# The last eight odd U chunks computed ahead, sixteen early gathers, and the gathered block closed at chunk 121

## The chip, the cores and the metric

The kernel runs on one core of a Trainium2 chip. The core has a matrix engine (TensorE, PE in the profile, PEld its weight loads), a vector engine (DVE), a scalar engine (ACT), GpSimd (POOL), and SP, which mostly issues DMA transfers. Each engine works through its own queue in order; semaphores make one wait for another. The metric is the time of one execution in microseconds (us) on the device.

## The reference, cut to what matters

One decoder block for 512 tokens of width 1024: attention and gated linear attention beside each other, then an expert layer, each behind a norm. The change touches the expert layer alone. For each token and each of 8 heads the 16 best of 16384 experts are picked (`expert`, `gates`), and

```
def block(args):
    xb, eb, gb = args                      # 128 tokens, 128 experts each
    ub = jnp.take(u, eb, axis=0)
    hid = jax.nn.gelu(jnp.einsum('tkd,td->tk', ub, xb)) * gb
    vb = jnp.take(v, eb, axis=0)
    return jnp.einsum('tk,tkd->td', hid, vb)
```

Behind it the result is scaled by a gate, added to the residual, normed and written out.

## The kernel before

The 512 tokens are four blocks of 128. Three of them (0, 1, 2) are computed **densely**: every expert for every token, with the gates as a matrix that is mostly zero. The fourth (`GB`, block 3) is computed by **gathers**: for each of its 128 places (16 experts of 8 heads) one indirect DMA fetches a row of `u` per token (gu) and one a row of `v` (gv).

The dense part goes through 128 chunks of 128 experts. For a chunk c there is

- a **U chunk** (`u_part`): ACT rounds the chunk of u to its high part (`uc..h`), DVE subtracts to get the low part (`uc..l`, called lo, L65), PE makes 24 matmuls of 128x368 into `ph` (L69 to L71; the last 16 of the 384 tokens take another way), ACT takes the gelu (L705) into `ge`.
- a **V chunk** (`v_part`, `v_matmuls`): ACT and DVE split v in the same way (`vc..h`, `vc..l`), DVE multiplies the gelu by the gates (L1169), ACT and DVE split the product into `Ah` (L1173) and `Al` (L1174), and PE adds 18 matmuls of 128x512 into the six accumulators `acc`.

The gelu of an odd chunk stays in SBUF (a ring of six) until its V chunk; that of an even chunk is written to DRAM (`gsp`) and read back for its V chunk (`gel`, two even chunks in one load).

Three stages follow each other after the front part (attention, mixers, query heads, to 403 us). In the **gate stage** (403 to about 714 us) PE builds the gate matrix from one-hot matrices (`pg`, L918) for the blocks one after the other, 8 places (q) to a block, and writes it to DRAM (`Gd`, read back as `gr`, eight chunks to a block of 1.5 MB). DVE is busy there with the one-hots. The 64 even U chunks (`AHEAD`) are woven in, by a running sum of the costs of DVE and PE. The first 8 gathers of u are done there too: each is issued at one place of the third block and its dot (`gather_u`, L1003) follows at the next. In the **V stage** (to 1503 us) each pair of V chunks has one odd U chunk, 8 chunks ahead (`LEAD`), until these are used up at chunk 119; the remaining gathers are spread evenly over chunks 0 to 123 (`gather_to`). The sum over gv is kept on DVE (`gacc`, L1016). After every eighth gu ACT takes the gelu of `hid` (L1006) and DVE multiplies it by the gates (hg, L1007). The last four V chunks (`LAST`) are done block by block, so that a block's accumulators are ready one after the other, and in the **tail** `finish` scales, adds, norms and writes each block (L1192 to L1203), the gathered block first.

The order of each engine's instructions is made ahead of time by a scheduler that simulates the program; DVE and POOL keep the written order in the gate stage, POOL also after it.

Of the kernel before, what the change touches and what calls it, by code (L numbers as in the profile page):

```python
# [46 lines left out]
def peer_block_kernel(ctx: ExitStack, tc: tile.TileContext, a: dict, out: bass.AP):  # L47
# [951 lines left out]
    def gather_u(s):  # L999
# [4 lines left out]
        if s % 8 == 7:  # L1004
            sl = slice(s - 7, s + 1)
            last_gelu["hg"] = nc.scalar.activation(hg[:, sl], hid[:, sl], AF.Gelu)  # L1006
            nc.vector.tensor_tensor(hg[:, sl], hg[:, sl], gg_g[:, sl], OP.mult)  # L1007
# [141 lines left out]
    def v_part(c):  # L1149
        if c % 2 == 0:  # L1150

            v_part.raw = dn.tile([P, 2, D], F32, tag="vraw", bufs=2, name=f"v{c}") if c else raw([P, 2, D], "v0")
            nc.sync.dma_start(v_part.raw, vPc[c:c + 2].rearrange("c i d -> i c d"))
        if c == 0:
            gates_of(0)
# [2 lines left out]
        if c % CG == 2 and c + CG < P:
# [2 lines left out]
        if c % 2 == 0:
            if c % 4 == 0:
                v_part.ge = dnA.tile([P, 2, TU], F32, tag="gel", bufs=2, name=f"gel{c}")
                nc.sync.dma_start(v_part.ge, gsp[c // 2:c // 2 + 2].rearrange("c p t -> p c t"))
            ge = v_part.ge[:, c // 2 % 2].rearrange("p (g t) -> p g t", g=NGU)
# [130 lines left out]
```

## Time and profile before

| | us |
|---|---|
| median of 3 runs | 1525.87 (1524.41 to 1526.83) |
| profiled execution | 1523.26 |
| its span | 1521.5 |
| front part and query heads | 0 to 403 |
| gate stage | 403 to 714 |
| V stage | 714 to 1503 |
| tail | 1503 to 1521.5 |

A time is that of the whole execution; the span runs from the first to the last instruction that the profiler recorded. In the profile an engine's busy share is over the whole span. A row of the timeline gives the start in us, the duration, engine, line, operation, tiles with their shapes, and in brackets how long the engine had been idle before and what ended it. A row of DMA issues gives the size and the median time from issue to landing.

### The profile page before, as it was taken

Reading aid. Unit: us, or ns where it says so; the run is one execution under the profiler, and the core shown is the slowest. Engines: PE = TensorE matmul, PEld = TensorE weight load, DVE = VectorE, ACT = ScalarE, POOL = GpSimd, SP = SyncE. Lnnn points to the kernel's source line nnn. Section 1 sums busy time; section 2 is a strip of 40 time slices with the busy share of each in tenths; the row PEclk is TensorE's granted clock in tenths of the full one; section 3 lists DMA queues with packets and bytes.
Section 4 is the critical chain, followed back from the end, with each engine's and each line's share of the span. In section 5 each row is a group of like instructions: output and inputs, shape, how many; then the busy total and the mean of one; then the engine's idle time right before and its main releaser. Section 6 shows DMA issues by size and latency. Waiting matters only on the chain.

```text
span 1521.5 us, 24401 instructions
## 1 busy us (share of the span) xinstructions
PE 1460.3 (96%) x9387; PEld 1301.7 (86%) x9387; DVE 1251.6 (82%) x2389; ACT 677.7 (45%) x1072; POOL 482.2 (32%) x344
## 2 busy tenths in 40 slices
PE   4999989899999999999999999999999999999995
PEld 3787877888999999999888888888888888888884
DVE  7578657689999999996778878787878878788998
ACT  5545486533344665765333333333333333333332
POOL 1000000145505220222334434453535434454461
PEclk9999999999999999999999999999999999999997
DMA  9253535462446997899999989989999898998894
GB/s 349 99 208 115 175 106 191 152 215 92 140 171 207 305 314 229 257 295 330 411 408 335 334 317 345 357 322 333 343 349 344 326 339 344 357 335 291 312 356 157
DMA packets 158004, 417.04 MB, mean 274 GB/s; under 512 B 11312, under 2 KB 78144, under 8 KB 145472
## 3 DMA queue, kind: packets, MB, share of 16 engines
q1 hardware_dynamic: 107296, 258.18, 47.5%
q0 software_dynamic: 39312, 144.20, 25.9%
q10 hardware_dynamic: 11280, 13.11, 2.5%
q8 instruction: 73, 1.20, 0.3%
q14 instruction: 43, 0.35, 0.1%
HBM read 374.01 MB, written 41.42 MB: 273 GB/s over the span
## 4 chain that ended last, share of the span: by engine, by line
PE 89%; DVE 4%; ACT 3%; DMA 2%; issue 2%; SPq 0%; DVEq 0%; POOL 0%; ACTq 0%; POOLq 0%
PE ph L71 11%; PE ph L69 11%; PE acc L70 11%; PE acc L69 11%; PE ph L70 11%; PE acc L71 11%; PE pg L918 4%; PE pq L69 2%; PE pq L71 2%; PE pq L70 2%; PE pj L71 1%; PE pj L69 1%; PE pj L70 1%; DMA gu<-in_u_dram,ix_u 1%; PE pn L69 1%
## 5 line engine op out<-in xcount | busy, mean ns | idle before, releaser
L993 POOL DMA_INDIRECT gu<-in_u_dram,ix_u x128 | 191.4, 1495 | 314.4 <-DVE gacc L1016 128.8
L1011 POOL DMA_INDIRECT gv<-in_vP_dram,ix_v x128 | 176.8, 1381 | 216.2 <-DVE gu L1003 163.9
L1173 ACT ACTIVATE Ah<-gr 128x384 fp32r<-128x384 f32 x128 | 67.1, 525 | 308.6 <-PE acc L70 305.0
L1016 DVE SCALAR_TENSOR_TENSOR gacc<-gv,hg,gacc 128x1024 f32<-128x1024 f32 x127 | 162.8, 1282 | 0.2
L1003 DVE SCALAR_TENSOR_TENSOR gu<-gu,h2n 128x1024 f32<-128x1024 f32 x128 | 156.0, 1220 | 0.7 <-DMA gu<-in_u_dram,ix_u 0.7
L705 ACT ACTIVATE ge<-ph 128x368 f32<-128x368 f32 x128 | 59.9, 468 | 152.8 <-PE ph L71 152.7
L1174 DVE TENSOR_TENSOR Al<-gr,Ah 128x384 fp32r<-128x384 f32 x128 | 71.0, 556 | 66.4 <-ACT Ah L1173 66.2
L920 ACT ACTIVATE gs<-pg 128x512 f32<-128x512 f32 x96 | 94.1, 1114 | 3.8 <-PE pg L918 2.8
L1066 POOL IOTA iot<- 128x256 bf16 x1 | 1.5, 1540 | 282.2 <-DVE h2Tl L680 282.2
L911 DVE TENSOR_TENSOR o<-o,gp 128x3072 bf16<-128x3072 bf16 x48 | 84.0, 1755 | 0.4 <-PE pg L918 0.4
L959 POOL DMA_INDIRECT spr<-in_u_dram,spix x16 | 40.6, 2535 | 105.6 <-DVE spr L964 61.3
L918 PE MATMUL pg<-o,o 128*128 128x128 bf16 x1152 | 72.7, 218 | 0.5 <-ACT gs L920 0.5
L918 PEld LDWEIGHTS <-o 128*128 128x128 bf16 x1152 | 66.2, 97 | 6.0 <-issue 0.7
L895 DVE TENSOR_TENSOR o<-iot,t 128x2048 bf16<-128x2048 bf16 x48 | 58.4, 1223 | 2.4 <-PE pg L918 2.4
L1169 DVE TENSOR_TENSOR gr<-ge,gr 128x368 f32<-128x368 f32 x64 | 34.5, 540 | 23.3 <-ACT ge L705 23.3
L217 DVE SCALAR_TENSOR_TENSOR macc<-wa,scs,macc 128x1024 f32<-128x1024 f32 x28 | 38.8, 1385 | 5.1 <-DMA wa<-in_w_ada_dram 4.8
L1169 DVE TENSOR_TENSOR gr<-gel,gr 128x368 f32<-128x368 f32 x64 | 31.9, 535 | 2.9 <-DMA gr<-Gd 2.9
L70 PE MATMUL pq<-h2Tl,wq_0h 128*128 128x512 f32 (+1 forms) x80 | 27.9, 349 | 1.2 <-DVE h2Tl L680 1.2
L69 PE MATMUL pq<-h2Th,wq_0h 128*128 128x512 f32 (+1 forms) x80 | 28.0, 352 | 1.0 <-ACT qha L758 1.0
L71 PE MATMUL pq<-h2Th,wq_1l 128*128 128x512 f32 (+1 forms) x80 | 28.1, 352 | 0.0
L70 PE MATMUL pq<-h2Tl,wq_1h 128*128 128x512 f32 (+1 forms) x80 | 28.1, 352 | 0.0
L69 PE MATMUL pq<-h2Th,wq_1h 128*128 128x512 f32 (+1 forms) x80 | 28.0, 350 | 0.0
(2608 smaller groups left out, 5028.3 us busy)
## 6 DMA issues: line engine op xcount, KB each, us to landing
u<-in_uT_dram SPq DMA_DIRECT2D x64, 1024.0 KB, 8.3
v<-in_vP_dram SPq DMA_DIRECT2D x64, 1024.0 KB, 7.5
Gd<-gs SPq DMA_DIRECT2D x23, 1024.0 KB, 8.1
gr<-Gd SPq DMA_DIRECT2D x15, 1536.0 KB, 11.0
wa<-in_w_ada_dram SPq DMA_DIRECT2D x20, 1024.0 KB, 6.3
gsp<-ge ACTq DMA_DIRECT2D x64, 184.0 KB, 4.6
gel<-gsp SPq DMA_DIRECT2D x32, 368.0 KB, 4.8
wi<-in_w_in_dram SPq DMA_DIRECT2D x9, 1024.0 KB, 6.2
```

The costliest lines, as they stand in the source:

```text
L69: nc.tensor.matmul(acc, lh, rh, start=start, stop=False)
L70: nc.tensor.matmul(acc, lh, rl, start=False, stop=False)
L71: return nc.tensor.matmul(acc, ll, rh, start=False, stop=stop)
L911: nc.vector.tensor_tensor(o2, o12[:, :, 1, None].to_broadcast([P, H, 3, P, 2]), gp3[:, g0:g0 + H, :, None].to_broadcast([P, H, 3, P, 2]), ...
L918: nc.tensor.matmul(pt[:, i, :], o12[:, g, 0, :, r], o2[:, g, m, :, r], start=(m == 0), stop=(m == 2))
L920: nc.scalar.activation(gs[:, :, t0 + 4 * f:t0 + 4 * f + 4].rearrange("p b a -> p a b"), pt, AF.Copy)
L993: nc.gpsimd.indirect_dma_start(out=ur, out_offset=None, in_=a["u"], in_offset=bass.IndirectOffsetOnAxis(ap=ix_u[:, s:s + 1], axis=0))
L1003: nc.vector.scalar_tensor_tensor(ur, ur, 1.0, h2n, op0=OP.mult, op1=OP.mult, accum_out=hid[:, s:s + 1])
L1011: nc.gpsimd.indirect_dma_start(out=vr, out_offset=None, in_=a["vP"], in_offset=bass.IndirectOffsetOnAxis(ap=ix_v[:, s:s + 1], axis=0))
L1016: nc.vector.scalar_tensor_tensor(gacc, vr, hg[:, s:s + 1], gacc, op0=OP.mult, op1=OP.add)
L1173: nc.scalar.activation(grp(Ah), A, AF.Copy)
L1174: nc.vector.tensor_tensor(grp(Al), A, grp(Ah), OP.subtract)
```

## The change

- Eight odd U chunks, 113, 115 to 127 (`ODD_AHEAD`, m = 28 to 31), join those computed ahead in the gate stage: 72 in place of 64. Their gelus are spilled to `gsp`, which is laid out anew, and read back as `gel1`.
- 16 gathers of u are done in the gate stage in place of 8. They are issued in pairs, at the last place of the second block and the first seven of the third; the two dots of a pair come one place later. The product hg of the first 16 is no longer made right behind ACT's gelu but at the next pair (`weigh`).
- The other gathers are spread over chunks 0 to 119 (`LAST_G`) in place of 0 to 123, by a cost of 4.0 for a V chunk of a pair with a U chunk and 2.3 for one of a pair without. The sum gv no longer starts ten places behind gu.
- The gathered block is closed (`finish(GB, ...)`), and ACT's table for the last norms loaded, at chunk 121, not behind the loop.
- The load of V chunk 0 and the first load of `gel` go to GpSimd's DMA queue, behind the first block of gates; they were on SP's.
- The load of the second block of gates is issued at chunk 4, no longer at chunk 2.

```diff
-AHEAD = tuple(range(0, P, 2))
+ODD_AHEAD = tuple(range(28, 32))
+AHEAD = tuple(c for m in range(P // 4) for c in (4 * m, 4 * m + 2) + ((4 * m + 1, 4 * m + 3) if m in ODD_AHEAD else ()))
...
-        if c % 2 == 0:
-            nc.scalar.dma_start(gsp[c // 2], gef)
+        if c in AHEAD:
+            nc.scalar.dma_start(gsp[c // 4, c % 2, c // 2 % 2], gef)
...
-    EARLY = 8
+    EARLY = 16
...
             last_gelu["hg"] = nc.scalar.activation(hg[:, sl], hid[:, sl], AF.Gelu)
+            waiting.append(sl)
+            if s >= EARLY:
+                weigh()
+
+    waiting = []
+
+    def weigh():
+        while waiting:
+            sl = waiting.pop()
             nc.vector.tensor_tensor(hg[:, sl], hg[:, sl], gg_g[:, sl], OP.mult)
...
-    VLAG = 10
-    gathers = [(s * 0.88 / NS, gather_u, s) for s in range(NS)]
-    gathers += [((s + VLAG) / (NS + VLAG), gather_v, s) for s in range(NS)]
+    gathers = [(-1, gather_u, s) for s in range(EARLY)]
+    gathers += [((s - EARLY) * 0.88 / (NS - EARLY), gather_u, s) for s in range(EARLY, NS)]
+    gathers += [((s + 0.5) / NS, gather_v, s) for s in range(NS)]
...
-    third_block = {0: [ahead(0, 1)]}
-    for q in range(1, EARLY):
-        third_block[q] = [dots_of(q - 1, 1), ahead(q, 1)]
-    third_block[EARLY - 1] += [dots_of(EARLY - 1, 1)]
+    third_block = {}
+    places = [(second_block, q) for q in range(7, 8)] + [(third_block, q) for q in range(P // TG)]
+    for i, (block, q) in enumerate(places):
+        pieces = block.setdefault(q, [])
+        if i:
+            pieces.append(dots_of(2 * i - 2, 2))
+        if i < EARLY // 2:
+            pieces.append(ahead(2 * i, 2))
...
+            if c == 0:
+                gates_of(0)
             v_part.raw = dn.tile([P, 2, D], F32, tag="vraw", bufs=2, name=f"v{c}") if c else raw([P, 2, D], "v0")
-            nc.sync.dma_start(v_part.raw, vPc[c:c + 2].rearrange("c i d -> i c d"))
-        if c == 0:
-            gates_of(0)
+            (nc.sync if c else nc.gpsimd).dma_start(v_part.raw, vPc[c:c + 2].rearrange("c i d -> i c d"))
...
-        if c % CG == 2 and c + CG < P:
+        if c % CG == (2 if c > CG else 4) and c + CG < P:
...
-                v_part.ge = dnA.tile([P, 2, TU], F32, tag="gel", bufs=2, name=f"gel{c}")
-                nc.sync.dma_start(v_part.ge, gsp[c // 2:c // 2 + 2].rearrange("c p t -> p c t"))
+                v_part.ge[c % 2] = dn.tile([P, 2, TU], F32, tag=f"gel{c % 2}", bufs=2 - c % 2, name=f"gel{c}")
+                (nc.sync if c else nc.gpsimd).dma_start(v_part.ge[c % 2], gsp[c // 4, c % 2].rearrange("c p t -> p c t"))
...
-    LEAD = 8
+    LEAD, LAST_G = 8, 120
+    share = [4.0 if c + 1 + LEAD < P and c + 1 + LEAD not in AHEAD else 2.3 for c in range(0, P, 2)]
+    cost = [share[c // 2] for c in range(LAST_G)]
...
-        if c % 2 == 0 and c + 1 + LEAD < P:
+        if c % 2 == 0 and c + 1 + LEAD < P and c + 1 + LEAD not in AHEAD:
             u_part(c + 1 + LEAD)
...
-        gather_to(len(gathers) * (c + 1) // (P - LAST))
+        weigh()
+        gather_to(EARLY + int((len(gathers) - EARLY) * sum(cost[:c + 1]) / sum(cost) + 1e-6))
+        if c == LAST_G + 1:
+            with tc.issue_after(last_gelu["u"].ins), tc.issue_after(last_gelu["hg"].ins):
+                nc.scalar.preload_act_table_set("natural_log_exp_and_others")
+            finish(GB, [gacc[:, 0:512], gacc[:, 512:1024]])
...
-    with tc.issue_after(last_gelu["u"].ins), tc.issue_after(last_gelu["hg"].ins):
-        nc.scalar.preload_act_table_set("natural_log_exp_and_others")
-    finish(GB, [gacc[:, 0:512], gacc[:, 512:1024]])
```

The order in which the engines take their work moves at three places.

ACT at the transition from the gate stage to the V stage, before (`ge9` is the gelu of the last U chunk ahead of the V stage, a name's last number only tells tiles apart):

```order
L705 ACTIVATE ge9_8344<-ph9_8319 128x368
L64 ACTIVATE vc0h_8350<-v0_8346 128x1024
L1173 ACTIVATE Ah0_8357<-gr0_8348 128x384
L64 ACTIVATE vc1h_8379<-v0_8346 128x1024
L1173 ACTIVATE Ah1_8384<-gr0_8348 128x384
```

and with the change:

```order
L706 ACTIVATE ge9_8633<-ph9_8608 128x368
L65 ACTIVATE vc0h_8639<-v0_8637 128x1024
L65 ACTIVATE vc1h_8675<-v0_8637 128x1024
L65 ACTIVATE uc11h_8708<-u9_8602 128x1024
L65 ACTIVATE vc2h_8741<-v2_8739 128x1024
L1189 ACTIVATE Ah0_8646<-gr0_8635 128x384
L1189 ACTIVATE Ah1_8680<-gr0_8635 128x384
```

Ah0, which PE's first V matmul reads, has three more operations ahead of it; PE has two matmuls of U chunk 11 between U chunk 9 and that first V matmul.

DVE in the chunks without U, from the lo of chunk 115 to that of chunk 116, with the change (L1185 is the product with the gates, L1190 Al, L1026 gacc, L1004 a dot):

```order
L66 TENSOR_TENSOR vc115l_14323<-v114_14288,vc115h_14322 128x1024
L1190 TENSOR_TENSOR Al117_14397<-gr14_14012,Ah117_14396 128x384
L1185 TENSOR_TENSOR gr15_14290<-gel120_14492,gr15_14290 128x23x16 x2
L1185 TENSOR_TENSOR gr15_14290<-gel124_14634,gr15_14290 128x23x16 x2
L1185 TENSOR_TENSOR gr15_14290<-gel121_14521,gr15_14290 128x23x16 x2
L1004 SCALAR_TENSOR_TENSOR gu124_13910,hid_2439<-gu124_13910,h2n_2430 128x1024
L1190 TENSOR_TENSOR Al118_14429<-gr14_14012,Ah118_14428 128x384
L1026 SCALAR_TENSOR_TENSOR gacc_8473<-gv109_13940,hg_2440,gacc_8473 128x1024
L1004 SCALAR_TENSOR_TENSOR gu125_13943,hid_2439<-gu125_13943,h2n_2430 128x1024
L1026 SCALAR_TENSOR_TENSOR gacc_8473<-gv110_13977,hg_2440,gacc_8473 128x1024
L1190 TENSOR_TENSOR Al119_14459<-gr14_14012,Ah119_14458 128x384
L1004 SCALAR_TENSOR_TENSOR gu126_14007,hid_2439<-gu126_14007,h2n_2430 128x1024
```

Twelve rows (fifteen operations) stand here between two lo subtractions; the products of chunks 120, 121, 122, 123, 124 and 126 are made in one go, four chunks or more ahead of their use.

ACT in the tail, before (rf1y and rf2y are the roots of blocks 1 and 2, L81 and L82 a logarithm and an exponential, y1 the rows of block 1):

```order
L81 ACTIVATE rf1y_14741<-rf1m_14740 128x1
L82 ACTIVATE rf1y_14741<-rf1y_14741 128x1
L81 ACTIVATE rf2y_14791<-rf2m_14790 128x1
L82 ACTIVATE rf2y_14791<-rf2y_14791 128x1
L1200 ACTIVATE y1_14730<-y1_14730,rf1y_14741 128x512 x2
```

and with the change:

```order
L82 ACTIVATE rf1y_14757<-rf1m_14756 128x1
L83 ACTIVATE rf1y_14757<-rf1y_14757 128x1
L82 ACTIVATE rf2y_14807<-rf2m_14806 128x1
L1218 ACTIVATE y1_14746<-y1_14746,rf1y_14757 128x512 x2
L83 ACTIVATE rf2y_14807<-rf2y_14807 128x1
```

The scaling of y1 now stands ahead of the last step of block 2's root.

More of the change, by code (lines that the diff above doesn't have):

```diff
@@ L687, in second_norm @@
                 nc.scalar.activation(h2n[:, half * 512:(half + 1) * 512], pb, AF.Copy)
-    gsp = dr.tile([len(AHEAD), P, TU], F32, name="gsp")
+    gsp = dr.tile([P // 4, 2, 2, P, TU], F32, name="gsp")
     ges, last_gelu = {}, {}
@@ L1105, in peer_block_kernel @@
                     6: [gate_parts(SB)], 7: [gate_rest(SB)]}
-    third_block = {0: [ahead(0, 1)]}
-    for q in range(1, EARLY):
-        third_block[q] = [dots_of(q - 1, 1), ahead(q, 1)]
-    third_block[EARLY - 1] += [dots_of(EARLY - 1, 1)]
+    third_block = {}
[6 more added lines that the diff above has]
+            pieces.append(ahead(2 * i, 2))
+    assert EARLY == 2 * len(places) - 2
     work = chain(route_heads(), *head, woven(0, rows, first_block), woven(1, rows, second_block),
@@ L1112, in peer_block_kernel @@
     NL_U = len(AHEAD) - LAST_U
-    DVE_ALL = 11 + 4 * 7.6 + 3 + 1.15 * TS + 2.82 * 2 * NGRP + 9 + 1.14 * (NL_U - WQ_U)
+    DVE_ALL = 11 + 4 * 7.6 + 3 + 1.15 * TS + 2.82 * 2 * NGRP + 1.15 * EARLY + 1.14 * (NL_U - WQ_U)
     PE_ALL = 1.4 * 2 * NGRP + 3 + UCOST * (NL_U - WQ_U)
@@ L1150, in v_part @@
         if c % 2 == 0:
+            if c == 0:
+                gates_of(0)
             v_part.raw = dn.tile([P, 2, D], F32, tag="vraw", bufs=2, name=f"v{c}") if c else raw([P, 2, D], "v0")
[L1153 to L1155 removed]
+            (nc.sync if c else nc.gpsimd).dma_start(v_part.raw, vPc[c:c + 2].rearrange("c i d -> i c d"))
         if c % CG == 0:
             v_part.g = gates_of.next
[L1158 removed]
+        if c % CG == (2 if c > CG else 4) and c + CG < P:
             gates_of(c // CG + 1)
         vh, vl = hilo(v_part.raw[:, c % 2], [P, D], f"vc{c}", nc.vector)
[L1161 to L1165 removed]
+        if c in AHEAD:
+            if c % 4 < 2:
+                v_part.ge[c % 2] = dn.tile([P, 2, TU], F32, tag=f"gel{c % 2}", bufs=2 - c % 2, name=f"gel{c}")
+                (nc.sync if c else nc.gpsimd).dma_start(v_part.ge[c % 2], gsp[c // 4, c % 2].rearrange("c p t -> p c t"))
+            ge = v_part.ge[c % 2][:, c // 2 % 2].rearrange("p (g t) -> p g t", g=NGU)
         else:
@@ L1175, in v_part @@
         return c, Ah, Al, vh, vl
+    v_part.ge = {}
     def v_matmuls(parts, blocks=range(len(DENSE)), qs=(0, 1)):
@@ L1214, in peer_block_kernel @@
         v_matmuls([parts])
-        gather_to(len(gathers) * (c + 1) // (P - LAST))
+        weigh()
+        gather_to(EARLY + int((len(gathers) - EARLY) * sum(cost[:c + 1]) / sum(cost) + 1e-6))
[3 more added lines that the diff above has]
+            finish(GB, [gacc[:, 0:512], gacc[:, 512:1024]])
         if c == 16:
```

## The prediction

> **What bounds the kernel now.** I read the page first, for the engine that fills the span; then the chain of waits; then the windows, one per stage, since the shares are means over stages with different limits; then the waits of TensorE (PE).
>
> ```profile
> span 1521.5 us, 24401 instructions
> PE 1460.3 (96%) x9387; PEld 1301.7 (86%) x9387; DVE 1251.6 (82%) x2389; ACT 677.7 (45%) x1072; POOL 482.2 (32%) x344
> PE 89%; DVE 4%; ACT 3%; DMA 2%; issue 2%; SPq 0%; DVEq 0%; POOL 0%; ACTq 0%; POOLq 0%
> ...
> 403.00:714.30 311.30, 309.48 (x2601) 303.28 (x2600) 289.35 (x446) 181.23 (x234) 73.18 (x40) 1.00 0.79 255
> 714.30:734.40 20.10, 20.10 (x122) 19.89 (x120) 7.48 (x12) 4.28 (x7) 8.47 (x9) 1.00 1.01 413
> 734.40:736.40 2.00, 0.10 (x1) 0.00 (x0) 0.96 (x2) 1.87 (x4) 0.00 (x0) 1.00 1.02 406
> 736.40:740.90 4.50, 4.49 (x13) 3.54 (x14) 4.50 (x7) 4.04 (x6) 1.68 (x1) 0.62 1.03 418
> 742.40:1438.00 695.60, 695.60 (x3412) 612.16 (x3412) 570.19 (x748) 251.66 (x355) 305.93 (x217) 1.00 0.92 342
> 1438.00:1452.00 14.00, 12.67 (x65) 10.55 (x64) 13.63 (x17) 5.40 (x8) 8.25 (x7) 1.00 0.82 299
> 1470.00:1480.00 10.00, 10.00 (x45) 8.26 (x44) 9.40 (x11) 3.61 (x6) 7.20 (x5) 1.00 0.99 364
> 1480.00:1490.00 10.00, 10.00 (x46) 8.28 (x45) 9.58 (x10) 3.77 (x5) 3.79 (x3) 1.00 1.01 377
> ...
> PE acc L69 <- ACT Ah L1173: 1.9, 1, 1.9
> PE acc L69 <- ACT vc118h L64: 1.3, 1, 1.3
> PE ph L71 <- DVE uc124l L65: 1.0, 1, 1.0
> ```
>
> PE carries 89% of the chain. A window gives its length, then busy time of PE, PE's loads, DVE, ACT and POOL, granted clock, DMA share and GB/s. From the gate stage (403 us) on PE stands still in few places: 1.8 us of the 311.3 before 714.3, of which the last row's 1.0 is one wait; 1.9 us at the transition, where the first V chunk waits for ACT's Ah; 1.3 us near 1450. The change leaves the number of matmuls alone, so all it can win from the stages is these 5 us, and it wins nothing where it only moves a matmul.
>
> **The swap of eight U chunks: 0.**
>
> ```profile
> 733.83 0.33 PE L69 MATMUL ph<-h2Th,uc9h 128*128 128x368 f32 x1
> 734.00 0.33 PE L70 MATMUL ph<-h2Tl,uc9h 128*128 128x368 f32 x1
> ...
> 1502.44 0.39 PE L70 MATMUL acc<-vc127l,Ah 128*128 128x512 f32 x1
> 1502.67 0.39 PE L71 MATMUL acc<-vc127h,Al 128*128 128x512 f32 x1
> ```
>
> U matmuls start 0.167 us apart, V matmuls 0.226: a U chunk is 24 x 0.167 = 4.0 us, a V chunk 18 x 0.226 = 4.08. Eight U chunks leave the V stage and come back in the gate stage: -32 + 32. Their lo subtractions, gelus, the eight spills on ACT's queue and the reads on SP's stay under PE in stages where ACT is at 58% (181.23 of 311.3) or less.
>
> **Gate stage: -1.0 (from -1.8 to +2).** It gains 32 us of PE, and on DVE eight lo subtractions and eight gather dots, 8 x 1.13 + 8 x 1.15 = 18.2 us (rows below; operations on DVE overlap by 0.09, a dot has a small read behind it). DVE's share falls from 289.35 / 311.3 = 93% to 307.6 / 343.3 = 90%. The one large stall goes:
>
> ```profile
> 705.53 0.17 DVE L1007 TENSOR_TENSOR hg<-hg,gg_g 128x8 f32<-128x8 f32 x1 [3.26 <-ACT hg L1006]
> 705.62 1.22 DVE L65 TENSOR_TENSOR uc124l<-u,uc124h 128x1024 fp32r<-128x1024 f32 x1
> 706.75 1.22 DVE L65 TENSOR_TENSOR uc126l<-u,uc126h 128x1024 fp32r<-128x1024 f32 x1
> ...
> gu<-in_u_dram,ix_u POOLq DMA_INDIRECT x10, 7.8
> ...
> L1003 DVE SCALAR_TENSOR_TENSOR gu<-gu,h2n 128x1024 f32<-128x1024 f32 x128 | 156.0, 1220 | 0.7 <-DMA gu<-in_u_dram,ix_u 0.7
> ```
>
> DVE stood 3.26 us at the small hg product, with three lo subtractions queued behind it and PE behind those. The product is now made one place later, when ACT's gelu is long done, so I take that 1.0; all 1.8 is the lower end. What is late next is a gather: two are issued per place and their dots come one place (10.8 us of PE) later, against 7.8 us median from issue to landing. The slack is 3 us for a median, so one or two late landings of a microsecond are the upper end.
>
> **Transition to the V stage: +2.5 (from +2.0 to +4.2).**
>
> ```profile
> 734.53 0.48 ACT L705 ACTIVATE ge<-ph 128x368 f32<-128x368 f32 x1 [3.52 <-PE ph L71]
> 734.90 1.05 ACT L64 ACTIVATE vc0h<-v 128x1024 fp32r<-128x1024 f32 x1
> 735.85 0.51 ACT L1173 ACTIVATE Ah<-gr 128x384 fp32r<-128x384 f32 x1
> 736.26 1.05 ACT L64 ACTIVATE vc1h<-v 128x1024 fp32r<-128x1024 f32 x1
> ...
> 736.41 2.41 PE L69 MATMUL acc<-vc0h,Ah 128*128 128x512 f32 x6 [1.92 <-ACT Ah L1173]
> ```
>
> Before, ACT does vc0h, then Ah0, and PE starts 0.56 us after Ah0 does. In the new order vc1h, uc11h and vc2h stand between the two: three operations at 0.95 us from start to start (734.90 to 735.85). Ah0 begins at 738.70 and PE's first V matmul at 739.26, 2.85 later. PE does two matmuls of U chunk 11 in that wait (0.33), so 2.5 is lost. The upper end adds the clock: 0.62 over 4.5 us cost 0.38 x 4.5 = 1.7 us after the present wait, and the longer one, broken by two matmuls, may cost it again.
>
> The Trainium skill ("TensorE: Matmul & The Clock Gate", Part 1, the HAM clock gate) says that the clock is either full or half and that a busy-watching window of about 3.4 us decides. The 0.62 agrees with it: 3.4 of 4.5 us at half speed give a mean of 0.62. By the rule an idle stretch over a second window doubles the loss, an estimate of 3.4 us in place of 1.7; the row bears out only one.
>
> **V chunk 0 and its gel on GpSimd's queue: 0 (up to +4.3).**
>
> ```profile
> gr<-Gd POOLq DMA_DIRECT2D x1, 1536.0 KB, 9.8
> v<-in_vP_dram SPq DMA_DIRECT2D x1, 1024.0 KB, 25.2
> ```
>
> In the 20 us before the transition the 16 DMA engines are full (share 1.01). The gate block on GpSimd's queue landed in 9.8 us there, 157 KB a microsecond; SP's v load, among six others, took 25.2. The two loads now moved (1024 and 368 KB) stand behind gr0 alone; at gr0's pace they take 8.9 us more, so both land near 733 at the latest, and vc0h can't start before 734.90. SP is spared them. If v0 took SP's 25.2 us from 714 on, it would land at 739.2, 4.3 late.
>
> **V chunks without U, 104 to 127: +0.5 (from -1.3 to +8).** Before, U chunks run until chunk 119; now every chunk from 104 on has only its own 4.08 us of PE to hide DVE and DMA.
>
> ```profile
> 1488.06 1.23 DVE L65 TENSOR_TENSOR vc126l<-v,vc126h 128x1024 fp32r<-128x1024 f32 x1 [0.39 <-ACT vc126h L64]
> 1489.20 1.28 DVE L1016 SCALAR_TENSOR_TENSOR gacc<-gv,hg,gacc 128x1024 f32<-128x1024 f32 x1
> 1490.40 1.22 DVE L65 TENSOR_TENSOR vc127l<-v,vc127h 128x1024 fp32r<-128x1024 f32 x1
> 1491.53 5.25 DVE L1016 SCALAR_TENSOR_TENSOR gacc<-gv,hg,gacc 128x1024 f32<-128x1024 f32 x4
> ...
> L1174 DVE TENSOR_TENSOR Al<-gr,Ah 128x384 fp32r<-128x384 f32 x128 | 71.0, 556 | 66.4 <-ACT Ah L1173 66.2
> ```
>
> From lo of chunk 104 to that of 127 DVE has, in the new order, 29 gacc x 1.20, 13 dots x 1.15, 23 lo x 1.13, 22 Al and 17 products at about 0.46 (0.56 less the overlap of 0.09), and 1.3 of small ones: 95 us. PE has 23 x 4.08 + 1.95 = 95.8. Nothing is left between them. Adding the order up chunk by chunk, DVE comes 0.2 to 1.4 us late before chunks 116, 120 and 124: three stalls of 0.6, +1.8, against the 1.3 near 1450, which goes with its U chunk. DMA has as little room: 42 gathers of 512 KB, 12 MB of v, 4 MB of gel and gates, some 38 MB in 95 us, 400 GB/s. The rows give 364 and 377 at a share of 1.0, and 418 in one short window. At 418 it fits; at 364 it takes 104 us, +8. I take the near end since DMA can be ahead of use by the ring's seven gathers.
>
> **Tail: +1.6 (from -2 to +3).** PE ends at 1503.06 (call it E).
>
> ```profile
> 1504.10 1.28 DVE L1192 TENSOR_TENSOR y<-acc,h2n 128x512 f32<-128x512 f32 x2
> 1505.42 1.28 DVE L1193 TENSOR_TENSOR y<-y,xl 128x512 f32<-128x512 f32 x2
> 1512.74 3.43 DVE L1203 SCALAR_TENSOR_TENSOR y<-y,rf2y,fwb 128x512 f32<-128x512 f32 x2
> ...
> 1511.88 1.33 ACT L1200 ACTIVATE y<-y,rf1y 128x512 f32<-128x512 f32 x2
> ```
>
> The gathered block is closed earlier in the program, yet DVE's order still has its sums after lo of chunk 127. PE's last matmuls are mixed otherwise: 15 follow the end of the first accumulator, not 25, so it is ready at E - 3.4 in place of E - 5.7. From there DVE has twelve half-row operations at 0.6, two final multiplies (together 1.33, as ACT's) and small ones: done at E + 5.4, before at E + 3.6 (1506.7). Then ACT takes block 1's scaling (1.33) ahead of the last step of block 2's root. Some of the 3.1 is hidden by the root chain; I take about half. The other end is the four gacc (5.25 us) gone from DVE's last 15 us: -2.
>
> **Sum.** -1.0 + 2.5 + 0.5 + 1.6 = +3.6. The profiled execution took 1523.26 us (span 1521.5 and 1.8 around it); that gives 1526.9. The median, 1525.87, stands 2.6 above that execution, so 1529.5 in the measure of the runs. A change under 0.2%, 3.05 us, can't be told from none.
>
> **Rivals.**
>
> (A) The gains eat the loss: all 1.8 of the gate stage and the 1.3 near 1450 come back, nothing new stalls, the tail is as long as before: 2.5 - 1.8 - 1.3 = -0.6, 1525.3. For it: DVE at 9.4 and 9.58 of 10 us in the two windows to 1490 cost PE nothing. Against it: that held for 20 us, not 95.
>
> (B) DMA sets the pace of the last 24 chunks at 364 GB/s: +8 in place of +0.5, 1537. For it: share 1.0 in those windows at that rate. Against it: 418 in another.
>
> (C) Faster: the tail loses the four gacc and y3's work, -2, beside A's gains and a transition of only +2.0: -3.1, and 1522.8; a gate stage with even more slack adds little, about 1522. Against it: y3's place in DVE's order.
>
> (D) V chunk 0 late: +4.3 more, 1533.8. For it: SP's 25.2; against it: gr0's 9.8. The Trainium skill ("DMA: Bandwidth & Descriptors", Issuing engines are not separate DMA queues) says that loads of every issuer end on the same 16 engines and that another issuer saves only the time to issue. By that rule v0 is no better off than SP's loads and D holds; the 9.8 beside 25.2 speaks against it, though gr0 was also issued ahead.
>
> **How the numbers follow.** Forecast 0.42, with its own range 1527 to 1532; A 0.26, B 0.12, C 0.15, D 0.05. Faster is most of C and a little of A: 0.17. Within 0.2% (1522.8 to 1528.9) is the rest of these and over a third of the forecast: 0.41. Slower: 0.42. The range leaves out the slower half of B and the faster half of C: 1522.5 to 1537.
>
> **What would show it.** Transition: Ah0 fourth after vc0h, and a PE wait near 4.4 us in two parts. Gate stage: no wait of hg, none of gu over 1 us. From chunk 104: PE waits at lo or Al of 116, 120, 124; a DMA share near 1.0 there for 90 us. Tail: the last final multiply ending at E + 14.5. The forecast fails if PE stands over 4 us between chunks 104 and 127, or if ACT does Ah0 right behind vc0h.

## The result: slower by 0.93%

| | us |
|---|---|
| before | 1525.55 median (1524.41 to 1526.83, 4 runs) |
| with the change | 1540.02 median (1535.74 to 1542.38, 4 runs) |
| ratio | 1.0093, 95% interval 1.0076 to 1.0110 |
| forecast | 1529.5, range 1522.5 to 1537.0 |

The direction was forecast, the size was not: +14.5 us where +3.6 was expected, and the time lies outside the range.

### The profile page after: what moved, and what is told of

It reads as the page before. It is cut to its first block, busy times and chain, and to the rows that moved or that the text cites. A ratio compares the mean times of both kernels' runs of the same rounds, so it can differ in the third digit from the quotient of the medians.

```text
span 1540.6 us, 24429 instructions
## 1 busy us (share of the span) xinstructions
PE 1473.5 (96%) x9387; PEld 1304.5 (85%) x9387; DVE 1252.8 (81%) x2389; ACT 678.6 (44%) x1072; POOL 472.0 (31%) x346
## 4 chain that ended last, share of the span: by engine, by line
PE 90%; DVE 3%; DMA 2%; ACT 2%; issue 1%; SPq 0%; ACTq 0%; DVEq 0%; POOL 0%; POOLq 0%
PE acc L71 12%; PE acc L70 12%; PE acc L72 11%; PE ph L70 11%; PE ph L72 11%; PE ph L71 11%; PE pg L919 4%; PE pq L70 2%; PE pq L72 2%; PE pq L71 2%; PE pj L70 1%; PE pj L72 1%; PE pj L71 1%; PE pn L70 1%; PE pn L71 1%
## 5 line engine op out<-in xcount | busy, mean ns | idle before, releaser
L994 POOL DMA_INDIRECT gu<-in_u_dram,ix_u x128 | 185.1, 1446 | 316.2 <-DVE gacc L1026 160.8
L1021 POOL DMA_INDIRECT gv<-in_vP_dram,ix_v x128 | 170.8, 1334 | 224.2 <-DVE gu L1004 178.6
L1026 DVE SCALAR_TENSOR_TENSOR gacc<-gv,hg,gacc 128x1024 f32<-128x1024 f32 x127 | 162.9, 1283 | 0.7 <-DMA gv<-in_vP_dram,ix_v 0.5
L1004 DVE SCALAR_TENSOR_TENSOR gu<-gu,h2n 128x1024 f32<-128x1024 f32 x128 | 155.6, 1219 | 6.6 <-DMA gu<-in_u_dram,ix_u 6.6
L1190 DVE TENSOR_TENSOR Al<-gr,Ah 128x384 fp32r<-128x384 f32 x128 | 71.0, 557 | 66.6 <-ACT Ah L1189 66.0
L912 DVE TENSOR_TENSOR o<-o,gp 128x3072 bf16<-128x3072 bf16 x48 | 84.0, 1753 | 12.8 <-PE pg L919 12.4
L1185 DVE TENSOR_TENSOR gr<-ge,gr 128x368 f32<-128x368 f32 x56 | 30.0, 539 | 25.1 <-ACT ge L706 14.6
L1185 DVE TENSOR_TENSOR gr<-gel,gr 128x368 f32<-128x368 f32 x72 | 35.5, 535 | 0.5 <-DMA gel<-gsp 0.5
```

The lines of the kernel that those rows point to most:

```text
L912: nc.vector.tensor_tensor(o2, o12[:, :, 1, None].to_broadcast([P, H, 3, P, 2]), gp3[:, g0:g0 + H, :, None].to_broadcast([P, H, 3, P, 2]), ...
L994: nc.gpsimd.indirect_dma_start(out=ur, out_offset=None, in_=a["u"], in_offset=bass.IndirectOffsetOnAxis(ap=ix_u[:, s:s + 1], axis=0))
L1004: nc.vector.scalar_tensor_tensor(ur, ur, 1.0, h2n, op0=OP.mult, op1=OP.mult, accum_out=hid[:, s:s + 1])
L1021: nc.gpsimd.indirect_dma_start(out=vr, out_offset=None, in_=a["vP"], in_offset=bass.IndirectOffsetOnAxis(ap=ix_v[:, s:s + 1], axis=0))
L1026: nc.vector.scalar_tensor_tensor(gacc, vr, hg[:, s:s + 1], gacc, op0=OP.mult, op1=OP.add)
L1190: nc.vector.tensor_tensor(grp(Al), A, grp(Ah), OP.subtract)
```

## The profile after

The page of the changed kernel, its windows by stage (columns as before: length, busy time of PE, PE's loads, DVE, ACT, POOL, granted clock, DMA share, GB/s), and PE's waits behind the gate stage:

```profile
span 1540.6 us, 24429 instructions
PE 1473.5 (96%) x9387; PEld 1304.5 (85%) x9387; DVE 1252.8 (81%) x2389; ACT 678.6 (44%) x1072; POOL 472.0 (31%) x346
...
403.00:748.80 345.80, 345.80 (x2823) 340.01 (x2823) 313.01 (x502) 195.50 (x254) 82.30 (x49) 1.00 0.81 261
768.90:774.90 6.00, 1.10 (x4) 0.55 (x3) 4.00 (x7) 4.89 (x7) 0.93 (x1) 0.67 1.02 407
774.90:779.20 4.30, 4.30 (x13) 3.50 (x14) 4.30 (x7) 1.14 (x3) 0.00 (x0) 0.66 1.03 398
779.20:1399.00 619.80, 619.80 (x3006) 539.90 (x3005) 503.95 (x656) 220.72 (x313) 267.35 (x194) 1.00 0.91 339
1448.90:1470.00 21.10, 18.45 (x79) 14.48 (x78) 19.88 (x28) 8.62 (x12) 10.41 (x9) 1.00 0.99 382
1470.00:1521.50 51.50, 51.24 (x228) 41.23 (x226) 47.63 (x59) 18.66 (x30) 18.42 (x13) 1.00 0.74 266
...
PE ph L70 <- ACT uc11h L65: 4.5, 1, 4.5
PE acc L70 <- ACT vc116h L65: 1.3, 1, 1.3
PE acc L70 <- ACT vc112h L65: 1.3, 1, 1.3
```

PE has the same 9387 instructions as before and is busy 13 us longer with them: 1473.5 against 1460.3; 11.0 of the 13 lie behind the end of U chunk 0. Waits are not the main thing: from the transition on they come to 7.8 us, before to 3.2. In the long V stage PE is busy without a gap in both kernels, at a full clock, and yet takes longer. The times at which PE ends a chunk show where the two part:

| PE ends | before | change | difference | of it, this part | predicted |
|---|---|---|---|---|---|
| U chunk 0 | 299.55 | 304.28 | 4.73 | front: 4.7 | 0 |
| U chunk 9 | 734.49 | 768.96 | 34.47 | gate stage, less 32 for its 8 more U chunks: -2.3 | -1.0 |
| V chunk 2 | 754.66 | 792.66 | 38.00 | transition: +3.5 | +2.5 |
| V chunk 101 | 1357.19 | 1403.15 | 45.96 | V chunks 3 to 101: +8.0 | 0 |
| last matmul | 1503.06 | 1521.52 | 18.46 | to the end, less the 32 given back: +4.5 | +0.5 |
| span | 1521.49 | 1540.62 | 19.13 | tail: +0.7 | +1.6 |

The front is the same code in both. Its end differs from run to run: U chunk 0 ended anywhere from 298.33 to 306.22 in the traces of this case, whatever the kernel, so the 4.7 is no effect of the change. The profiled execution, 1542.38, is also the slowest of the four, and 14.4 us are left to explain, about the difference of the medians.

The largest part, 8.0, sits where the prediction had put nothing. PE's timeline of V chunks 42 and 43 and the first matmul of the U chunk behind them, before:

```profile
994.63 0.40 PE L69 MATMUL acc<-vc42h,Ah 128*128 128x512 f32 x1
...
998.76 0.39 PE L69 MATMUL acc<-vc43h,Ah 128*128 128x512 f32 x1
...
1002.84 0.33 PE L69 MATMUL ph<-h2Th,uc53h 128*128 128x368 f32 x1
```

and with the change:

```profile
1035.79 0.39 PE L70 MATMUL acc<-vc42h,Ah 128*128 128x512 f32 x1
...
1039.97 0.39 PE L70 MATMUL acc<-vc43h,Ah 128*128 128x512 f32 x1
...
1044.16 0.33 PE L70 MATMUL ph<-h2Th,uc53h 128*128 128x368 f32 x1
```

The two V chunks take 4.13 + 4.08 us before and 4.18 + 4.19 with the change. The matmuls, their order and their waits are the same. Over all V matmuls the mean time from one start to the next is 227.9 ns before and 232.5 with the change, within 1 ns of that in nearly every stretch of 8 chunks; for U matmuls it is 166.8 and 166.6. Over 2304 V matmuls the difference (4.63 ns before rounding) is 10.7 us.

## Experiments: the pace of the V matmuls

What differs for a V matmul is where its operands lie. In `acc<-vc42h,Ah` a slice of Ah (or Al) is the stationary operand, the weights that are loaded, and the high or low part of v is the moving one. The change puts gel into another pool (`dn` in place of `dnA`) and gives it a third tile, gel1, 2944 bytes of each partition. That pool is laid out up to the top of SBUF, the core's on-chip memory, so what lies ahead of gel1 slides down by 2944 bytes, Ah and Al among it: from byte 192224 of each partition to 189280 (the places are those that the built kernel gives its tiles). The parts of v stay at 88032 and up. Two kernels move Ah and Al and nothing else that these matmuls read; the order of every engine stays the same.

In the changed kernel, gel1's place is taken ahead of Ah:

```diff
     v_part.ge = {}
+    gel_pre = dn.tile([P, 2, TU], F32, tag="gel1", bufs=1, name="gelpre")
```

> The changed kernel with one tile (gel1, 2944 bytes of each partition) placed ahead of Ah instead of last, so that Ah and Al lie at byte 192224 of each partition as in the kernel before, not at 189280 as in the changed one. The order of every engine is unchanged. What is to be told: in the V stage of the changed kernel a V matmul starts 232.5 ns after the last one, 227.9 ns in the kernel before; over 2304 V matmuls that is 10.7 us. Theory A (where Ah and Al lie sets the pace): V matmuls back at about 228 ns, the time near 1540 - 10.7 = 1529. Rival B (what runs beside them, DMA or DVE, sets it, or the run): pace stays at 232.5 and the time at 1540.

In the kernel before, an unused tile is put at the end of the pool:

```diff
+    dn.tile([P, 2, TU], F32, tag="pad", bufs=1, name="pad")
     xl = dn.tile([P, 2, D], F32, tag="vraw", bufs=2, name="xl")
```

> The kernel before with an unused tile of 2944 bytes at the end of the same pool, which moves Ah and Al from byte 192224 down to 189280, where the changed kernel has them (and v and the gather tiles with them). Order of every engine unchanged, nothing else changed. Theory A (place): V matmuls at about 232.5 ns from start to start and 1525.6 + 10.7 = 1536. Rival B (neighbours or the run): 228 ns and 1525.6, no difference.

Measured: 1528.98 us for the first (ratio to before 1.0041, 1.0025 to 1.0057) and 1534.76 for the second (1.0063, 1.0046 to 1.0080; before in the same job 1523.50). The same three rows, first of the changed kernel with Ah put back, then of the kernel before with Ah moved down:

```profile
1029.23 0.40 PE L70 MATMUL acc<-vc42h,Ah 128*128 128x512 f32 x1
...
1033.36 0.39 PE L70 MATMUL acc<-vc43h,Ah 128*128 128x512 f32 x1
...
1037.44 0.33 PE L70 MATMUL ph<-h2Th,uc53h 128*128 128x368 f32 x1
```

```profile
1001.36 0.39 PE L69 MATMUL acc<-vc42h,Ah 128*128 128x512 f32 x1
...
1005.53 0.39 PE L69 MATMUL acc<-vc43h,Ah 128*128 128x512 f32 x1
...
1009.73 0.33 PE L69 MATMUL ph<-h2Th,uc53h 128*128 128x368 f32 x1
```

The paces have changed hands: 4.13 + 4.08 with the change, 4.17 + 4.20 in the kernel before; means 227.8 and 232.5 ns. Theory A holds: the engines do the same work in the same order beside the matmuls, and the pace goes with the place alone (rival B falls). Of the 14.5 us, 10.7 by the pace (7.9 and 9.6 by the ratios of the two kernels) come from a detail of the layout that no instruction shows.

Four pads of other sizes in the kernel before ask what about the place counts (32 columns of 4 bytes, then 64, 96 and 768):

```diff
+    dn.tile([P, 32], F32, tag="pad", bufs=1, name="pad")
     xl = dn.tile([P, 2, D], F32, tag="vraw", bufs=2, name="xl")
```

> The kernel before, with 128 unused bytes in place of the 2944 of the run before: Ah at byte 192096. Read is the start-to-start time of V matmuls alone (227.9 ns in the kernel before, 232.5 with 2944 bytes). Theory A1 (the remainder of Ah's place by some power of two from 256 up counts): the remainder by 256 is now that of the slow layout (96; 224 before), so slow if 256 counts, and fast or slow if 512. Rival A2 (the distance, or the region that Ah and Al lie in, counts): 128 bytes change nothing, 228 ns.

> As above with 256 unused bytes, Ah at byte 191968: the remainder by 256 is the fast one (224), by 512 a third one (480). A1 by 256: 228 ns. A1 by 512: neither the fast nor the slow remainder, open. A2: 228 ns.

> As above with 384 unused bytes, Ah at byte 191840: the remainders by 256 and 512 are both those of the slow layout (96 and 352). A1: 232.5 ns. A2: 228 ns.

> As above with 3072 unused bytes, Ah at byte 189152, only 128 bytes from the slow layout: the remainders by 256, 512 and 1024 are those of the kernel before (224, 224, 736). A1: 228 ns. A2: 232.5 ns, as at 189280.

Measured, one run each, before 1524.49: 1534.64, 1524.05, 1535.20 and 1522.21 us, at 232.5, 227.9, 232.5 and 227.9 ns. 128 unused bytes cost 10 us; 3072 cost nothing. The remainder by 256 counts, and distance or region don't. All four buffers of Ah and of Al have the same remainder, since they are 1536 = 6 x 256 bytes long.

Is it Ah's remainder alone, or Ah's against that of v's parts? In the kernel before both are 224; the parts of v get there by 48 unused columns behind `hg`. Making these 80 moves the parts (they are also the stationary operand of U matmuls) to remainder 96:

```diff
-    hg = h2p.tile([P, P + 48], F32, name="hg")[:, :P]
+    hg = h2p.tile([P, P + 80], F32, name="hg")[:, :P]
```

> The kernel before with hg's unused columns 32 longer, so that the four tiles of high and low parts (the moving operand of V matmuls and the stationary one of U matmuls) lie 128 bytes higher: remainder by 256 is 96 in place of 224. Ah and Al stay at 192224 (remainder 224). Order unchanged. Theory S (the stationary operand's place alone counts, 96 slow): V matmuls 228 ns, U matmuls slower than 166.7. Theory M (stationary and moving operand must have the same remainder): V matmuls 232.5 ns, about 1534.

The next one has both shifts of 128 bytes (that edit and the pad of 32 columns), the two after it pads of 24 and 56 columns alone:

> The kernel before with both shifts of 128 bytes: the high and low parts (moving operand of V, stationary of U) and Ah, Al (stationary of V) have remainder 96 by 256. With the moving parts alone shifted, V matmuls took 233.3 ns and U matmuls 168.7. Theory M (the two operands of a matmul have to agree): V matmuls back at 228 ns, U matmuls still 168.7 (their moving operand did not move): about 1525 + 3072 x 1.9 ns = 1531. Theory S (a stationary operand at 96 is slow by itself): V 232.5 or slower, U 168.7, 1541.

> The kernel before with 96 unused bytes: Ah at 192128, remainder 128 by 256; the moving parts stay at 224. If it is enough that both lie in the same half of 256 bytes: 228 ns. If the remainders have to be equal: slower than 228.

> The kernel before with 224 unused bytes: Ah at 192000, remainder 0 by 256, a multiple of every power of two to 512; the moving parts stay at 224. Same half theory: 232.5 ns, since 0 and 224 lie in different halves. If alignment of the stationary operand is what counts: 228 ns or less.

Measured, one run each: 1541.38 (before 1525.72), then 1533.98, 1535.16 and 1534.47 (before 1526.24). Mean times from start to start, worked out from all rows of PE's timeline in the V stage:

| matmul | stationary, remainder by 256 | moving | ns | in |
|---|---|---|---|---|
| V | 224 | 224 | 227.9 | before; pads 256, 3072; change with Ah put back |
| V | 96 | 96 | 227.9 | both shifted |
| V | 96 | 224 | 232.5 | the change; pads 128, 384, 2944 |
| V | 128 | 224 | 233.1 | pad 96 |
| V | 0 | 224 | 233.3 | pad 224 |
| V | 224 | 96 | 233.3 | moving parts shifted |
| U | 224 | 32 | 166.8, 166.6 | before, the change |
| U | 96 | 32 | 168.8, 169.0 | moving parts shifted, both shifted |

Theory S falls (96 against 96 is fast), and so does the idea that an aligned stationary operand is best (0 is among the slowest). For V both layouts with equal remainders are fast and all four unequal ones that were tried are slow, as theory M said; the same half of 256 bytes is not enough (128 against 224). U shows that the rule isn't quite that: 224 against 32 is unequal and at least as good as any U pace seen. Why the relation matters, and what the full rule is, stays open.

## Experiments: the other four microseconds

**The transition.** ACT's timeline in the changed kernel, and GpSimd's issue of the loads:

```profile
769.00 0.48 ACT L706 ACTIVATE ge<-ph 128x368 f32<-128x368 f32 x1 [3.50 <-PE ph L72]
770.49 1.06 ACT L65 ACTIVATE vc0h<-v 128x1024 fp32r<-128x1024 f32 x1 [1.01 <-DMA v<-in_vP_dram]
771.45 1.04 ACT L65 ACTIVATE vc1h<-v 128x1024 fp32r<-128x1024 f32 x1
772.40 1.04 ACT L65 ACTIVATE uc11h<-u 128x1024 fp32r<-128x1024 f32 x1
773.35 1.04 ACT L65 ACTIVATE vc2h<-v 128x1024 fp32r<-128x1024 f32 x1
774.29 1.74 ACT L1189 ACTIVATE Ah<-gr 128x384 fp32r<-128x384 f32 x4
...
755.55 0.58 POOL L1162 DMA_DIRECT2D gr<-Gd  x1 [24.39 <-DMA gsp<-ge]
756.12 0.75 POOL L1171 DMA_DIRECT2D v<-in_vP_dram  x1
```

Ah0 is the fifth operation behind the gelu, as the order said. On top of that V chunk 0 is 1.0 us late: its load could be issued only at 756.12, behind the gates (gr0), which by the profile had waited for the last spills (gsp); that is 12.8 us before U chunk 9 ended, and vc0h, which waits for it, began 14.4 us after the issue. One kernel gives both loads back to SP's queue, a second does so with Ah put back; ACT's order then has Ah0 right behind vc0h:

```diff
-            (nc.sync if c else nc.gpsimd).dma_start(v_part.raw, vPc[c:c + 2].rearrange("c i d -> i c d"))
+            nc.sync.dma_start(v_part.raw, vPc[c:c + 2].rearrange("c i d -> i c d"))
...
-                (nc.sync if c else nc.gpsimd).dma_start(v_part.ge[c % 2], gsp[c // 4, c % 2].rearrange("c p t -> p c t"))
+                nc.sync.dma_start(v_part.ge[c % 2], gsp[c // 4, c % 2].rearrange("c p t -> p c t"))
```

> The changed kernel with one part undone: V chunk 0 and the first gel are loaded on SP's queue again. ACT's order at the transition is then that of the kernel before (Ah0 right behind vc0h). Theory (the order of ACT costs the transition 3.5 us): PE's wait before the first V matmul falls from 4.9 us to about 2, and the time to about 1540 - 3 = 1537, the V matmuls staying at 232.5 ns. Rival (the loads are late on SP's queue, as its 25 us for v say): the wait stays at 4 us or more, 1540.

> Both of the above at once: Ah and Al at byte 192224, V chunk 0 and the first gel on SP's queue. If the two causes are separate and add up: 1540 - 10.7 - 3 = 1526, no different from the kernel before. If the pace isn't set by the place of Ah: 1537.

Measured: 1539.85 (1.0113, 1.0094 to 1.0132) and 1528.34 (1.0029, 1.0018 to 1.0040). By the intervals neither is told apart from its partner (1.0093 and 1.0041). In the traces PE's wait for Ah0 is back to 1.9 us in both, but the gain is eaten: in the first DVE makes PE wait 2.3 us more for vc0l; in the second PE waits earlier, at U chunk 3, behind a spill whose issue holds ACT for 7 us, and then runs 3.4 us at half clock:

```profile
742.85 7.04 ACTq L708 DMA_DIRECT2D gsp<-ge  x1
...
PE ph L70 <- ACT ge L706: 1.9, 1, 1.9
PE acc L70 <- ACT Ah L1189: 1.9, 1, 1.9
```

So ACT's order was costed rightly, but undoing it alone brings nothing that can be measured. One spill's issue takes 3.9 us in the changed kernel too; the longest in the kernel before is 0.35. Odd chunks are not its condition: with the 16 early gathers alone (below), which spill no odd chunk, one issue takes 4.4 us. What holds it up is not shown.

**Parts alone.** Three parts of the change, each put alone into the kernel before, with Ah at 192224. The early gathers and hg:

```diff
-    EARLY = 8
+    EARLY = 16
...
+            waiting.append(sl)
+            if s >= EARLY:
+                weigh()
...
+    places = [(second_block, q) for q in range(7, 8)] + [(third_block, q) for q in range(P // TG)]
...
```

> The kernel before with one part of the change alone: 16 early gathers in pairs, the product hg put off by a place, gv no longer ten places behind gu. Ah stays at 192224. In the changed kernel the gate stage was 2.3 us shorter than the 32 us of its eight more U chunks ask for. If that comes from this part (no wait at hg): PE's waits of 1.0 and 0.5 us in the gate stage are gone and the time is 1 to 2 us below before. If it comes from having more U chunks to weave: no difference.

The end of the gathers:

```diff
...
-        gather_to(len(gathers) * (c + 1) // (P - LAST))
+        gather_to(int(len(gathers) * sum(cost[:c + 1]) / sum(cost) + 1e-6))
+        if c == LAST_G + 1:
+            ...
+            finish(GB, [gacc[:, 0:512], gacc[:, 512:1024]])
...
```

> The kernel before with one part alone: the gathers end at chunk 120, paced by the costs 4.0 and 2.3, and the gathered block is closed at chunk 121. Ah stays at 192224. My reading: the tail gets no shorter, since DVE has y3 behind its last lo in any case, and ACT's order at its end is that of before: within 1.5 us of before. Rival C of the prediction (the sums and y3 leave the tail): 2 us less.

The odd chunks ahead:

```diff
-AHEAD = tuple(range(0, P, 2))
+ODD_AHEAD = tuple(range(28, 32))
+AHEAD = tuple(c for m in range(P // 4) for c in (4 * m, 4 * m + 2) + ((4 * m + 1, 4 * m + 3) if m in ODD_AHEAD else ()))
...
```

> The kernel before with one part alone: the eight odd U chunks 113 to 127 computed ahead (their gel1 tile lies ahead of Ah, so that Ah stays at 192224). Order at the transition is that of before. If the swap is neutral as the prediction has it: the gate stage 32 us longer, the V stage 32 us shorter, and within 1.5 us of before. If the V chunks without U are short of DVE or DMA time, as the two waits of 1.3 us in the changed kernel say: 2 to 4 us slower, with waits at chunks 112 and 116.

| part alone | us | ratio | gate stage | last matmul to end of span |
|---|---|---|---|---|
| before | 1525.72 | | | 18.4 |
| 16 early gathers | 1527.70 | 1.0013 (0.9995 to 1.0030) | +9.2 | 12.0 |
| gathers end at 120 | 1523.84 | 0.9995 (0.9984 to 1.0006) | +0.4 | 15.3 |
| odd chunks ahead | 1550.08 | 1.0165 (1.0132 to 1.0197) | +1.7 beside the 32 | 29.2 |
| the change, Ah put back | 1528.98 | 1.0041 | -2.3 beside the 32 | 19.2 |

(The gate stage is the time from the end of U chunk 0 to that of U chunk 9, against before.) None of the three is neutral, and they lean on each other. With the early gathers alone DVE is busy for 303.70 of 324 us of the gate stage (94%), and PE waits in many small places and runs 3.4 us at half clock; with eight more U chunks to hide the gathers the stage comes out shorter. The odd chunks alone take the cover of 32 us from the gathers at the end: from V chunk 102 on PE loses 7.8 us and the tail is 10.8 longer. DVE is still adding gathers 4 us behind the last matmul, and waits for their landing:

```profile
1514.91 3.93 DVE L1017 SCALAR_TENSOR_TENSOR gacc<-gv,hg,gacc 128x1024 f32<-128x1024 f32 x3
1519.10 1.28 DVE L1017 SCALAR_TENSOR_TENSOR gacc<-gv,hg,gacc 128x1024 f32<-128x1024 f32 x1 [0.27 <-DMA gv<-in_vP_dram,ix_v]
1521.20 1.28 DVE L1017 SCALAR_TENSOR_TENSOR gacc<-gv,hg,gacc 128x1024 f32<-128x1024 f32 x1 [0.82 <-DMA gv<-in_vP_dram,ix_v]
```

(PE's last matmul ended at 1518.01 there.) With all three parts together (last row) that loss is gone again, but the tail is not below that of before. That the pacing to chunk 120 does this is likely, since it leaves 15.3 alone, but no run has the pacing and the odd chunks without the early gathers.

**The waits near chunks 112 and 116.** The prediction expected PE to wait for DVE here. It waits for ACT:

```profile
1444.66 0.53 ACT L1189 ACTIVATE Ah<-gr 128x384 fp32r<-128x384 f32 x1 [3.66 <-PE acc L71]
1448.78 0.52 ACT L1189 ACTIVATE Ah<-gr 128x384 fp32r<-128x384 f32 x1 [3.59 <-PE acc L71]
1449.21 1.04 ACT L65 ACTIVATE vc112h<-v 128x1024 fp32r<-128x1024 f32 x1
```

ACT stands idle 3.59 us, then makes Ah and then vc112h, which PE needs at once. ACT's order tells why: that Ah is the one of chunk 115, the fourth in a ring of four, and its buffer is that of chunk 111, which PE reads until it has ended chunk 111. An Ah three chunks ahead that stands in front of a high part makes PE wait through both: 1.3 us. Read from the orders alone, this holds ahead of chunk 118 before, 112 and 116 with the change, 118 and 119 with the gathers ending at 120, 112, 116, 120 and 124 with the odd chunks alone, and nowhere among the late chunks with the 16 early gathers alone. The waits of 1.3 to 1.4 us in the traces are at just these chunks, but for one: in the kernel with the odd chunks alone PE waits ahead of 116 for DVE's dg (2.8 us; dg feeds g2b, matmuls that spread the last gate over the partitions). That ACT's order is the cause is read from orders that differ in other things too; no run moved an Ah alone. Where a U chunk lies between (chunk 12 in some of the kernels) it covers the wait.

**Versions meant to beat both.** The changed kernel with Ah put back, the loads on SP's queue, and the gathers ended earlier:

```diff
-    LEAD, LAST_G = 8, 120
+    LEAD, LAST_G = 8, 112
```

> A version that may beat both: the changed kernel with Ah at 192224, the first loads of v and gel on SP's queue, and the gathers paced to end at chunk 112, the gathered block closed at 113 (LAST_G = 112). With LAST_G = 120 this was 0.3% slower than before. If DVE's work for the gathers in the chunks without U sets what is left (waits of 1.3 us at chunks 112 and 116, a tail no shorter): these waits go and the tail loses some 3 us, so 4 to 6 us less, 1522 or a little under before. If the transition and the gate stage set it: no difference from LAST_G = 120.

1528.43 us (1.0014, 1.0002 to 1.0026): a little better than with 120 (1.0029), the intervals overlapping, and not below before. The waits at 112 and 116 stayed, as ACT's order now says they must (it holds it ahead of 124 as well, where g2b's matmuls lie between); the tail fell to 17.4 us. Two more, with the same end of the gathers, without odd chunks and with 8 early gathers in pairs, or with two odd chunks and 16:

```diff
-ODD_AHEAD = tuple(range(28, 32))
+ODD_AHEAD = tuple(range(32, 32))
...
-    EARLY = 16
+    EARLY = 8
...
-    places = [(second_block, q) for q in range(7, 8)] + [(third_block, q) for q in range(P // TG)]
+    places = [(third_block, q) for q in range(3, P // TG)]
```

> A version that may beat both: no odd chunk ahead and 8 early gathers as before, in pairs with the hg product put off; the gathers paced to end at chunk 112 and the gathered block closed at 113; Ah at 192224; loads of v and gel on SP's queue. In DVE's order the gathered block is then wholly done before the first accumulator is ready, as in the run with 16 early gathers alone, whose tail was 12.0 us (18.5 before). If the tail follows from that: 6 us less there; the gate stage 1 us less (hg); ACT's order has Ah of 121 and 122 ahead of the high parts of chunks 118 and 119, two waits of 1.3 us in place of one: 1525.5 - 6 - 1 + 1.3 = 1520. If the gathers pressed into 112 chunks stall PE instead (DVE at 86% there, DMA at 0.95): no gain.

```diff
-ODD_AHEAD = tuple(range(28, 32))
+ODD_AHEAD = tuple(range(31, 32))
```

> As the version above with 16 early gathers and two odd chunks (125, 127) ahead. ACT's order has no Ah three chunks ahead of a high part, so no waits of 1.3 us; the tail as above, 12 us. The gate stage has 9.2 us more on DVE for the gathers and 8 us of PE with 2.3 us on DVE to cover it: with 16 early gathers alone it was 7.9 us longer; if the two U chunks cover 5.7 us of that, 2 us remain. 1525.5 - 6.4 - 1.3 + 2 = 1520. If the gate stage is as much longer as without the two chunks: 1526.

Both missed widely: 1545.98 (1.0135, 1.0119 to 1.0151) and 1540.09 (1.0090, 1.0075 to 1.0105); before 1525.15. PE's largest wait in each behind the front, first in the version without odd chunks, then in that with two:

```profile
PE g2b L1252 <- DVE dg L1247: 7.0, 1, 7.0
```

```profile
PE acc L70 <- ACT Ah L1189: 7.7, 2, 4.5
```

In the first, the matmuls of g2b stand in PE's queue among the last V chunks and need dg, which stands in DVE's queue behind the sums that had been pressed together; with its other late waits PE also ran 10.2 us at half clock. The waits of 1.3 us at 118 and 119 came as the order said, and none in the second; but 4.5 us went at Ah of chunk 123 in that one, and the tails were 16.2 and 17.0 us, not 12. That closing the gathered block early sets the tail is thus not shown. No version tried beats the kernel before.

## Why the prediction was wrong

**The step that failed** is the one called "The swap of eight U chunks: 0", with the sentence ahead of it that all the change can win from the stages is PE's idle time. It took the pace of a matmul, 0.226 us, as a constant that goes along when matmuls are moved (0.226 is that of the last chunks; the mean over the V stage was 0.228). The matmuls were the same, but the change moved their operands, and V matmuls went to 232.5 ns: +10.7 us over 2304 of them, the term missing from the sum. In the table by parts it is the +8.0 of V chunks 3 to 101 and some 2.4 of the +4.5 behind them (26 chunks x 18 x about 5.2 ns). No term, bound or rival held it, so the range couldn't reach it. With Ah put back the ratio is 1.0041 (1.0025 to 1.0057), +6.3 us, against the +3.6 forecast. In the profiled execution the rest without the pace is 14.4 - 10.7 = +3.7; that this meets +3.6 so closely is luck, since each term missed and the misses cancel, as the next paragraphs show.

**Gate stage**, -1.0 (to -1.8): -2.3. PE has no wait left there (345.80 of 345.80 us busy), and DVE none at hg, as read. But DVE does wait for gathers, 3.04 and 1.02 us, where none over 1 us was forecast; PE had work to go on with:

```profile
714.42 1.23 DVE L1004 SCALAR_TENSOR_TENSOR gu<-gu,h2n 128x1024 f32<-128x1024 f32 x1 [3.04 <-DMA gu<-in_u_dram,ix_u]
...
716.67 1.23 DVE L1004 SCALAR_TENSOR_TENSOR gu<-gu,h2n 128x1024 f32<-128x1024 f32 x1 [1.02 <-DMA gu<-in_u_dram,ix_u]
```

DVE's share is 313.01 / 345.8 = 91%, forecast 90%. That the stage gained more than PE's 1.8 us of idle time is not explained.

**Transition**, +2.5 (to +4.2): +3.5. ACT's order was as read. The rest is 1.0 of rival D, since v0 landed 1.0 us after ACT was free; behind PE's wait the clock cost no more than before (0.66 over 4.3 us, 1.5 us). With Ah put back, v0 landed in time, PE stood 4.2 us (4.4 forecast), and the clock made up the rest, towards the upper end of this term:

```profile
736.40:740.90 4.50, 4.49 (x13) 3.54 (x14) 4.50 (x7) 4.04 (x6) 1.68 (x1) 0.62 1.03 418
```

```profile
770.19:775.60 5.41, 5.41 (x13) 4.30 (x14) 5.41 (x10) 1.19 (x3) 0.00 (x0) 0.50 1.04 400
```

The first row is the kernel before behind its wait of 1.9 us, the second the changed kernel with Ah put back behind its two waits: half speed for all of 5.4 us, 2.7 us lost, and not 1.7. In all, half speed lasts 3.41 us in the trace of the kernel before, and 6.83 both with the change, where more than half of it came before the first V matmul, and with Ah put back. The rule of the Trainium skill that was weighed ("TensorE: Matmul & The Clock Gate", Part 1) agrees: half speed lasted two of its windows. But the loss is not certain. The kernel before with a pad of 256 bytes has the same wait of 1.92 us at this place and the full clock behind it:

```profile
738.80:743.30 4.50, 4.49 (x20) 3.72 (x21) 4.50 (x7) 4.50 (x8) 1.68 (x1) 1.00 1.02 416
```

So some 1.7 us of the difference between two profiles here can be chance.

**V chunk 0 on GpSimd's queue**, 0: the landing "near 733 at the latest" was wrong in its time base. It carried over the 21 us that lay between the issue of gr0 and V chunk 0 before; with the change gr0 waited, by the profile, for a spill (gsp, where it had been a store of Gd), was issued 13.4 us ahead of U chunk 9's end, and the margin was gone. ACT's spills had been held up by the issue of 3.9 us just before; whether that or the weaving of eight more U chunks took the margin is not separated.

**Chunks 104 to 127**, +0.5: without the pace some +2: inside the range, but four times the forecast, and for another cause. DVE stalled PE for 0.3 us (at vc116l) and DMA, at a share of 0.99 and 382 GB/s where PE waited most, not at all; ACT's order against the ring of four Ah did, by the reading above. The rows of the order that the document shows for this place have "Al117, Al118, Al119" between two lo; their Ah partners on ACT would have told it.

**Tail**, +1.6: +0.7. The last final multiply ended at 1534.86 + 1.42 = 1536.28, 14.8 us behind the last matmul (14.5 forecast, which is 1.4 above the 13.1 of before and not quite the sum's 1.6), with ACT's scaling ahead of the root as read:

```profile
1531.14 1.33 ACT L1218 ACTIVATE y<-y,rf1y 128x512 f32<-128x512 f32 x2 [0.23 <-issue]
1532.38 0.19 ACT L83 ACTIVATE rf2y<-rf2y 128x1 f32<-128x1 f32 x1
...
1534.86 1.42 DVE L1221 SCALAR_TENSOR_TENSOR y<-y,rf2y,fwb 128x512 f32<-128x512 f32 x2
```

What was forecast too large is the output behind it, 4.3 us in place of 5.3.

Of the prediction's rivals, B (DMA at its limit) and A did not come, and D came with 1.0 of its 4.3 us; C's gain in the tail is real for some orders (12.0 us with 16 early gathers alone) and not for this one.

## What to carry to other kernels

An edit that adds, drops or moves a tile also moves the tiles allocated around it, and here the place of an operand by 256 bytes was worth more than any wait that the edit was made for: where matmuls bound a kernel, compare the addresses of their operands before and after, and the time from one matmul's start to the next, before any other reading. When PE is busy longer with the same instructions, a kernel that moves only a pad settles it in one run. In an order made ahead of time, a ring buffer's write that stands in front of something the bounding engine needs at once is a wait that can be read off before the kernel runs.
